# RG-LRU gates as 64-row weight blocks on the two halves of TensorE's rows, in a hybrid decoder layer

## The chip, the cores and the metric

The kernel runs on one core of one Trainium2 chip. The metric is the device time of one execution in microseconds (us). Of the kernel before, three runs took 732.56, 734.33 and 735.61 us, so the median is 734.33 us. The execution that the profiler recorded took 734.08 us, of which the core's span (first to last recorded instruction) is 732.3 us. PE is the matrix engine TensorE, PEld its weight loads, DVE is VectorE, ACT is ScalarE, SP issues DMAs.

## The reference

One decoder layer on 512 tokens with 2048 features: a normalised and modulated input is projected to 4160 columns. Of these, 1024 go through a causal convolution of width 4 and a gated linear recurrence (RG-LRU), others through latent attention; both are multiplied with a SiLU gate, concatenated, projected back and added to the input. Cut to the part that the change touches:

```python
def rg_lru_branch(xr, conv_w, conv_b, w_rg_a, b_rg_a, w_rg_x, b_rg_x, lru_lambda):
    xc = causal_depthwise_conv(xr, conv_w) + conv_b          # 1024 channels
    xb = xc.reshape(B, S, RNN_BLOCKS, RNN_BLOCK)             # 16 blocks of 64 channels
    r = sigmoid(einsum('bshi,hij->bshj', xb, w_rg_a) + b_rg_a)
    i = sigmoid(einsum('bshi,hij->bshj', xb, w_rg_x) + b_rg_x)
    log_a = -LRU_C * r * softplus(-lru_lambda)
    a = exp(log_a)
    b = sqrt(-expm1(2.0 * log_a)) * (i * xc)
    h = linear_recurrence(a, b)                              # h[t] = a[t] h[t-1] + b[t]

def reference(...):
    h = rms_norm(x) * (1 + scale) + shift                    # scale, shift, gate from c
    xr, gr, qc, kvc, kr, ga = split(h @ w_in)
    y_rnn = rg_lru_branch(xr, ...) * silu(gr)
    y_att = mla_branch(qc, kvc, kr, ...) * silu(ga)
    return x + gate * (concat(y_rnn, y_att) @ w_out)
```

The gate weights are block diagonal: 16 blocks of 64 x 64 for r and as many for i, so each channel's gates depend on the 64 channels of its own block.

## The kernel before

Channels lie on the 128 partitions, tokens on the 512 columns of a tile. Every product of float32 matrices is made of three matmuls on values split in two (`mm3`, line 127): high part times high part, high times low, low times high. Splitting a tile costs one copy on ACT (the high part) and one subtraction on DVE (the low part), in `split`, line 120.

The input projection is done in four chunks of the 2048 input features (2, 3, 4 and 7 tiles of 128 features). The last chunk is the stage that the change lies in: the loop over `MORDER[:24]` calls `proj_last` for each of 24 output tiles. One call loads 128 x 896 weights (`wraw`, then split into `whi` and `wlo`, two buffers each in this stage), issues 21 matmuls of 512 columns (14 with `whi`, 7 with `wlo`) into one PSUM bank (`pp`), and DVE adds the bank to the partial sums of the earlier chunks. ACT writes `whi` for the next tile while PE works on the present one, and DVE writes `wlo` behind it.

Between these calls the recurrence is issued in two halves of four channel tiles. `rg_conv` (at n = 4, 5 and n = 9, 10) makes the convolution of a channel tile (`xc`), splits it (`xs`), loads and splits the gate weights (`graw`, `gh`, `gl`: 128 x 256, two block-diagonal 128 x 128 matrices, half of them zeros), makes six matmuls (`pr` and `pi`, one PSUM bank each, on banks 4 to 7 in turn), two sigmoids on ACT (r into the tile's own slot, i into `ig`), and the product `ig` times `xc` on DVE. `rg_decay` (n = 6 and 11) makes the decay with Exp and Tanh, `rg_scan` (n = 7 and 12) a square root and the scan. Sigmoid, Exp/Tanh and Sqrt are each behind an ACT table load, and `tab` keeps these functions in the order in which they are written.

A scheduler orders the instructions of PE, ACT and DVE within the program from its own estimates of time; SP's DMAs stay as written. So gate matmuls stand between projection matmuls at places that the scheduler chose, and ACT's and DVE's queues mix both kinds of work. Each engine works through its own row in order.

Of the kernel before, what the change touches and what calls it, by code (L numbers as in the profile page):

```python
# [12 lines left out]
F32 = mybir.dt.float32  # L13
F32R = mybir.dt.float32r
BF16 = mybir.dt.bfloat16
I32 = mybir.dt.int32
AF = mybir.ActivationFunctionType
# [3 lines left out]
P = 128  # L21
# [29 lines left out]
C_BADA, C_CW, C_CB, C_BA, C_BX, C_LAM, C_QA, C_KVA, NVEC = 0, 48, 80, 88, 96, 104, 112, 116, 120  # L51
# [33 lines left out]
def body(ctx, nc, tc, a):  # L85
# [3 lines left out]
    def act(out, in_, func, **kw):  # L89
        return A.activation(out=out, in_=in_, func=func, **kw)  # L90

    def tab(out, in_, func, **kw):
        if last_tab[0] is None:
            i = act(out, in_, func, **kw)
        else:
            with tc.issue_after(last_tab[0]):
                i = act(out, in_, func, **kw)
        last_tab[0] = i.ins if hasattr(i, "ins") else i
        return i

    def stt(out, in0, scalar, in1, op0, op1, **kw):
        return V.scalar_tensor_tensor(out=out, in0=in0, scalar=scalar, in1=in1, op0=op0, op1=op1, **kw)
# [14 lines left out]
    def tt(o, x, y, op):  # L117
        return V.tensor_tensor(out=o, in0=x, in1=y, op=op)  # L118

    def split(hi, lo, src):  # L120
        act(hi, src, AF.Copy)
        return tt(lo, src, hi.bitcast(F32), ALU.subtract)

    def mm(out, lhsT, rhs, start, stop, **kw):
        PE.matmul(out=out, lhsT=lhsT, rhs=rhs, start=start, stop=stop, **kw)  # L125

    def mm3(out, wh, wl, xh, xl, start, stop, **kw):
        mm(out, wh, xh, start, False, **kw)
        mm(out, wh, xl, False, False, **kw)
        mm(out, wl, xh, False, stop, **kw)  # L130
# [38 lines left out]
    def bank(kind, name):  # L169
        return psp.tile([P, S], F32, tag=f"b{next(cyc[kind])}", name=name)  # L170
# [31 lines left out]
    vec = cst.tile([P, NVEC], F32, name="vec")  # L202
# [347 lines left out]
    rg = rgctx.enter_context(tc.tile_pool(name="rg", bufs=1))  # L550
# [7 lines left out]
    def half(tags, cnt, cache, name):  # L558
        n = cnt[0]
        cnt[0] += 1  # L560
        if n % 2 == 0:
            cache[0] = bigt(tags[(n // 2) % len(tags)], name)
        return cache[0][:, n % 2]
# [3 lines left out]
    def tmp(name):  # L567
        return rg.tile([P, S], F32, tag="t", name=name, bufs=4)

    def rg_conv(m):  # L570
        w = lambda t: vec[:, C_CW + 8 * t + m:C_CW + 8 * t + m + 1]
        x = slot[XR + m]
        xc = half(XC, xcn, xcc, "xc")
        act(xc, x, AF.Identity, scale=w(3), bias=vec[:, C_CB + m:C_CB + m + 1])
        for s in (1, 2, 3):
            stt(xc[:, s:S], x[:, 0:S - s], w(3 - s), xc[:, s:S], ALU.mult, ALU.add)
        xs = rg.tile([P, 2, S], F32R, tag="xs", name="xs", bufs=2)
        xh, xl = xs[:, 0], xs[:, 1]
        split(xh, xl, xc)
        raw = rg.tile([P, 256], F32, tag="graw", name="graw", bufs=2)  # L580
        DMA.dma_start(out=raw, in_=a["wrg"][m])
        gh = rg.tile([P, 256], F32R, tag="gh", name="gh", bufs=2)
        gl = rg.tile([P, 256], F32R, tag="gl", name="gl", bufs=2)
        split(gh, gl, raw)
        pr = bank("aux", "pr")
        mm3(pr, gh[:, 0:P], gl[:, 0:P], xh, xl, True, True)
        pi = bank("aux", "pi")
        mm3(pi, gh[:, P:2 * P], gl[:, P:2 * P], xh, xl, True, True)
        tab(x, pr, AF.Sigmoid, bias=vec[:, C_BA + m:C_BA + m + 1])
        ig = tmp("ig")  # L590
        tab(ig, pi, AF.Sigmoid, bias=vec[:, C_BX + m:C_BX + m + 1])
        tt(xc, ig, xc, ALU.mult)
        return xc

# [104 lines left out]
    for n, m in enumerate(MORDER[:24]):  # L699
# [13 lines left out]
        if n in (4, 5):  # L713
            for t in (2 * n - 8, 2 * n - 7):
                xcs[t] = rg_conv(t)
# [6 lines left out]
        if n in (9, 10):  # L722
            for t in (2 * n - 14, 2 * n - 13):
                xcs[t] = rg_conv(t)
# [395 lines left out]
def _layout(x, c, positions, w_ada, b_ada, w_in, conv_w, conv_b, w_rg_a, b_rg_a, w_rg_x, b_rg_x, lru_lambda,  # L1120
            q_a_norm, w_uq, kv_a_norm, w_ukv, q_norm_nope, q_norm_rope, k_norm_nope, k_norm_rope, w_out):
    f = np.float32
    con = np.ascontiguousarray
    d = {}
    d["x"] = con(x[0].T).reshape(NK, P, S)
    d["xtok"] = con(x[0]).reshape(NT, P, D)
    d["c"] = con(c).reshape(4, S)
    d["pos"] = con(positions[0].reshape(NT, P).T)
    d["ada"] = con(w_ada[0].T).reshape(48, P, D)
    w = w_in[0]  # L1130
    cols = np.concatenate([w[:, 0:2048], w[:, 2048:2560], w[:, 2560:3072], w[:, 3136:4160]], axis=1)
    c4 = cols.reshape(NK, P, 32, P)
    c4 = c4[:, :, list(MORDER)]
    for ci, (k0, kc) in enumerate(CHUNKS):
        G = GROUP[ci]
        t = c4[k0:k0 + kc].reshape(kc, P, 32 // G, G, P)
        d[f"win{ci}"] = con(t.transpose(2, 1, 3, 0, 4)).reshape(32 // G, P, G * kc * P)
    kc = CHUNKS[0][1]
    d["winf"] = con(c4[:kc, :, :NF].reshape(kc, P, NF // 4, 4 * P).transpose(0, 2, 1, 3))
    kr4 = w[:, 3072:3136].reshape(NK, P, 64)  # L1140
    for ci, (k0, kc) in enumerate(CHUNKS):
        d[f"wkr{ci}"] = con(kr4[k0:k0 + kc].transpose(1, 0, 2)).reshape(P, kc * 64)
    g = np.zeros((8, P, 2, P), f)
    for m in range(8):
        for gi, wr in enumerate((w_rg_a[0], w_rg_x[0])):
            for b in range(2):
                g[m, b * 64:(b + 1) * 64, gi, b * 64:(b + 1) * 64] = wr[2 * m + b]
    d["wrg"] = g.reshape(8, P, 256)
    uk = w_ukv[0].reshape(2, 2, P, 4, 2, 2, P)
    t = uk.transpose(3, 0, 2, 1, 5, 4, 6)  # L1150
    d["wuk"] = con(t[:, :, :, :, 0].transpose(0, 2, 1, 3, 4, 5)).reshape(4, P, 1024)
    d["wuv"] = con(t[:, :, :, :, 1].transpose(0, 2, 1, 3, 4, 5)).reshape(4, P, 1024)
    uq = w_uq[0].reshape(2, 2, P, 4, 2, 192).transpose(3, 0, 2, 1, 4, 5)
    d["wqn"] = con(uq[..., 0:128].transpose(0, 2, 1, 3, 4, 5)).reshape(4, P, 1024)
    uq2 = w_uq[0].reshape(4, P, 4, 2, 192).transpose(2, 1, 0, 3, 4)
    d["wqp"] = con(uq2[..., 128:192]).reshape(4, P, 512)
    d["wlast"] = con(w_out[0][15 * P:, NACC * P:(NACC + 4) * P])
    d["wout"] = con(w_out[0].reshape(16, P, 16, P).transpose(2, 1, 0, 3)).reshape(16, P, 2048)
    v = np.zeros((P, NVEC), f)
    v[:, 0:48] = b_ada[0].reshape(48, P).T  # L1160
    v[:, C_CW:C_CW + 32] = conv_w[0].reshape(4, 8, P).transpose(2, 0, 1).reshape(P, 32)
    for col, arr in ((C_CB, conv_b), (C_BA, b_rg_a), (C_BX, b_rg_x), (C_LAM, lru_lambda)):
        v[:, col:col + 8] = arr[0].reshape(8, P).T
    for col, arr in ((C_QA, q_a_norm), (C_KVA, kv_a_norm)):
        v[:, col:col + 4] = arr[0].reshape(4, P).T
    d["vec"] = v
    r = np.zeros((P, NROW), f)
    for col, arr in ((R_QN, q_norm_nope), (R_KN, k_norm_nope), (R_QR, q_norm_rope), (R_KR, k_norm_rope)):
        r[:, col:col + arr.shape[1]] = arr[0][None, :]
    r[:, R_IF:R_IF + 32] = INV_FREQ[None, :]  # L1170
    r[:, R_ID:R_ID + P] = np.eye(P, dtype=f)
    r[:, R_MK:R_MK + P] = np.triu(np.full((P, P), -1e30, f), 1)
    d["row"] = r
    return d
# [14 lines left out]
```

## Time and profile before

| | |
|---|---|
| median of 3 runs | 734.33 us (732.56 to 735.61) |
| the profiled execution | 734.08 us, span 732.3 us |
| PE busy | 720.5 us, 98% of the span |
| PE weight loads busy | 597.4 us, 82% |
| DVE busy | 527.1 us, 72% |
| ACT busy | 353.6 us, 48% |
| gate matmuls | 48 of 128 x 512, from 255.6 to 299.6 us |
| gate sigmoids | 16 of 128 x 512, from 256.5 to 301.8 us |

A timeline row of the profile has the start in us, the length in us, the engine, the source line, the operation, what it writes and reads, its shape and how many such instructions were merged into the row; square brackets hold the idle time of the engine before the row and what ended it. Matmuls are pipelined: each is recorded with its latency (0.39 us at 512 columns), and the time that it costs is the distance of two starts. In a windows row each engine has its busy time in the stretch and its number of instructions.

### The profile page before, as it was taken

To read this page: it belongs to the slowest core of one execution; us is meant where nothing else is said; L and a number is where in the kernel's file an instruction comes from. 1 tells how busy PE (TensorE), PEld (TensorE's weight loads), DVE (VectorE), ACT (ScalarE), POOL (GpSimd) and SP (SyncE) were. 2 spreads that over 40 slices of the span, in tenths; PEclk is the share of its full clock that TensorE was granted. 3 is DMA by queue.
4 is the path that set the end of the run, shared out by engine and by line. 5 is a ranking of instruction groups with operands and counts; after the bars stand their busy time and mean duration, and the time that the engine had idled before them with its cause. 6 is when DMAs were issued, how large, how long until landed. Compare 5 with 4: busy or idle time off the path is not lost.

```text
span 732.3 us, 10065 instructions
## 1 busy us (share of the span) xinstructions
PE 720.5 (98%) x3625; PEld 597.4 (82%) x3626; DVE 527.1 (72%) x949; ACT 353.6 (48%) x728; POOL 29.4 (4%) x34
## 2 busy tenths in 40 slices
PE   9799999999999999999999999999999999999998
PEld 4588887788888888878888888888888877888887
DVE  2997878899998889897765566567686677783232
ACT  7366322231223489875545568677465434222221
POOL 0000000000000000001011111111120100000000
PEclk9899999999999999999999999999999999999999
DMA  8998366987822322223243315213433799774330
GB/s 308 391 409 323 116 242 225 368 325 272 332 80 79 127 80 81 81 79 101 82 134 95 93 59 202 62 55 118 130 127 100 239 333 296 241 228 138 114 94 29
DMA packets 46002, 127.94 MB, mean 175 GB/s; under 512 B 5373, under 2 KB 9341, under 8 KB 42369
## 3 DMA queue, kind: packets, MB, share of 16 engines
q1 hardware_dynamic: 38896, 106.34, 42.1%
q10 hardware_dynamic: 7056, 20.97, 8.5%
q8 instruction: 28, 0.46, 0.2%
q14 instruction: 22, 0.17, 0.1%
HBM read 123.10 MB, written 4.19 MB: 174 GB/s over the span
## 4 chain that ended last, share of the span: by engine, by line
PE 79%; DMA 7%; DVE 5%; ACT 5%; issue 3%; SPq 1%; POOLq 0%; POOL 0%; ACTq 0%; DVEq 0%
PE pp L125 36%; PE oa L125 23%; PE sc L125 4%; PE uwqn L125 3%; PE uwuk L125 3%; DMA ada<-in_ada 3%; PE uwuv L125 3%; DMA xtok<-in_xtok 2%; PE op L125 2%; PE uqp L125 2%; DMA wraw<-in_wout 1%; PE tp L894 1%; ACT pj L90 1%; PE tq L794 1%; DVE xc L118 1%
## 5 line engine op out<-in xcount | busy, mean ns | idle before, releaser
L125 PE MATMUL pp<-h,whi 128*128 128x512 f32 x992 | 242.0, 391 | 0.5 <-ACT h L90 0.5
L90 ACT ACTIVATE whi<-wraw 128x512 fp32r<-128x512 f32 (+4 forms) x172 | 126.8, 740 | 207.5 <-PE pp L125 69.7
L125 PEld LDWEIGHTS pp<-h,whi 128*128 128x128 f32 x992 | 184.8, 188 | 39.7 <-ACT whi L90 1.0
L118 DVE TENSOR_TENSOR wlo<-wraw,whi 128x512 fp32r<-128x512 f32 (+4 forms) x172 | 141.0, 822 | 67.6 <-ACT whi L90 35.9
L125 PE MATMUL pp<-h,wlo 128*128 128x512 f32 x496 | 127.2, 390 | 1.5 <-DVE wlo L118 1.5
L125 PEld LDWEIGHTS pp<-h,wlo 128*128 128x128 f32 x496 | 92.7, 188 | 21.6 <-DVE wlo L118 2.5
L125 PE MATMUL oa<-yh,whi 128*128 128x512 f32 (+1 forms) x272 | 102.4, 384 | 0.1
L125 PE MATMUL oa<-yl,whi 128*128 128x512 f32 (+1 forms) x272 | 102.3, 380 | 0.0
L276 DVE CUSTOM_DVE_ANT_0 ada<-ada,cb,vec 128x2048 f32<-128x2048 f32 (+1 forms) x32 | 70.7, 2211 | 11.3 <-DMA ada<-in_ada 11.3
L118 DVE TENSOR_TENSOR pj<-pp,pj 128x512 f32<-128x512 f32 x96 | 64.0, 683 | 13.8 <-PE pp L125 13.2
L125 PE MATMUL oa<-yh,wlo 128*128 128x512 f32 (+1 forms) x272 | 71.8, 380 | 0.0
L125 PEld LDWEIGHTS oa<-yl,whi 128*128 128x128 f32 x272 | 51.3, 189 | 8.9 <-DVE yl L118 0.2
L125 PEld LDWEIGHTS oa<-yh,whi 128*128 128x128 f32 x272 | 51.3, 189 | 8.8 <-ACT yh L90 0.3
L125 PEld LDWEIGHTS oa<-yh,wlo 128*128 128x128 f32 x272 | 49.1, 188 | 9.1
L90 ACT ACTIVATE h<-x,mod 128x512 fp32r<-128x512 f32 x14 | 10.2, 730 | 33.4 <-DVE mod L276 17.7
L125 PE MATMUL sc<-kT,qT 128*128 128x128 f32 (+3 forms) x96 | 22.8, 332 | 1.1 <-ACT kT L90 1.1
L90 ACT ACTIVATE pj<-pp 128x512 f32<-128x512 f32 x32 | 17.4, 611 | 9.3 <-PE pp L125 9.3
L90 ACT ACTIVATE pr<-sc,nm 128x128 f32<-128x128 f32 (+3 forms) x32 | 16.7, 521 | 10.6 <-DVE nm L886 10.4
L276 DVE CUSTOM_DVE_ANT_0 ada<-ada,cbo,vec 128x1024 f32<-128x1024 f32 x16 | 20.5, 1279 | 1.2 <-DMA ada<-in_ada 1.2
L229 POOL TENSOR_TENSOR hs<-hs,mhalf 128x8 f32<-128x8 f32 x12 | 21.2, 1768 | 1.0
L276 DVE CUSTOM_DVE_ANT_0 ada<-ada,cbo,modh 128x1024 f32<-128x1024 f32 x16 | 20.5, 1279 | 0.9 <-DMA ada<-in_ada 0.9
L125 PE MATMUL uwuv<-whi,kvt 128*128 128x256 f32 x80 | 20.8, 284 | 0.0
(222 smaller groups left out, 1001.6 us busy)
## 6 DMA issues: line engine op xcount, KB each, us to landing
ada<-in_ada SPq DMA_DIRECT2D x28, 1024.0 KB, 7.9
ada<-in_ada ACTq DMA_DIRECT2D x32, 512.0 KB, 4.9
wraw<-in_wout SPq DMA_DIRECT2D x59, 256.0 KB, 3.6
wraw<-in_win SPq DMA_DIRECT2D x22, 512.0 KB, 6.5
wraw<-in_win SPq DMA_DIRECT2D x24, 448.0 KB, 3.2
wraw<-in_win SPq DMA_DIRECT2D x16, 384.0 KB, 4.2
xtok<-in_xtok SPq DMA_DIRECT2D x8, 512.0 KB, 7.3
xo<-in_x SPq DMA_DIRECT2D x16, 256.0 KB, 4.9
```

Source lines behind the costliest of these rows:

```text
L90: return A.activation(out=out, in_=in_, func=func, **kw)
L118: return V.tensor_tensor(out=o, in0=x, in1=y, op=op)
L125: PE.matmul(out=out, lhsT=lhsT, rhs=rhs, start=start, stop=stop, **kw)
L229: G.tensor_tensor(out=out, in0=out, in1=mhalf[:, :n], op=ALU.pow)
L276: ttr_last[0] = V.tensor_tensor_reduce(out=t, in0=t, in1=cv, op0=ALU.mult, op1=ALU.add, scale=1.0, scalar=vec[:, C_BADA + j:C_BADA + j + 1 ...
L794: PE.transpose(tp[:, d * 256 + i2 * P:d * 256 + (i2 + 1) * P], kt[u][:, q * P:(q + 1) * P], ident)
L894: PE.transpose(tp[:, j * P:(j + 1) * P], pr[:, j * P:(j + 1) * P], ident)
```

## The change

The gate weights of a channel tile become 128 x 128: partitions 0 to 63 hold block 2m with its r columns and i columns side by side, partitions 64 to 127 hold block 2m+1 with its i columns first and then r. The six matmuls of a tile now have 64 rows of weights each: three on rows 0 to 63 of the array into bank `pg0` (r of the lower channels on partitions 0 to 63, i of the same channels on 64 to 127), three on rows 64 to 127 into bank `pg1` (i below, r above). They are issued in turn, one for each half. The two sigmoids of 128 partitions become four of 64 partitions; those of i read one half of the partitions and write the other, so that i lies again on its channels. The bias column of i is rolled by 64 partitions for that. Loads, splits and buffers of the gate weights are half as wide.

```diff
--- before.py
+++ after.py
@@ -577,18 +577,20 @@
         xs = rg.tile([P, 2, S], F32R, tag="xs", name="xs", bufs=2)
         xh, xl = xs[:, 0], xs[:, 1]
         split(xh, xl, xc)
-        raw = rg.tile([P, 256], F32, tag="graw", name="graw", bufs=2)
+        raw = rg.tile([P, P], F32, tag="graw", name="graw", bufs=2)
         DMA.dma_start(out=raw, in_=a["wrg"][m])
-        gh = rg.tile([P, 256], F32R, tag="gh", name="gh", bufs=2)
-        gl = rg.tile([P, 256], F32R, tag="gl", name="gl", bufs=2)
+        gh = rg.tile([P, P], F32R, tag="gh", name="gh", bufs=2)
+        gl = rg.tile([P, P], F32R, tag="gl", name="gl", bufs=2)
         split(gh, gl, raw)
-        pr = bank("aux", "pr")
-        mm3(pr, gh[:, 0:P], gl[:, 0:P], xh, xl, True, True)
-        pi = bank("aux", "pi")
-        mm3(pi, gh[:, P:2 * P], gl[:, P:2 * P], xh, xl, True, True)
-        tab(x, pr, AF.Sigmoid, bias=vec[:, C_BA + m:C_BA + m + 1])
+
+        pb = [bank("aux", f"pg{b}") for b in range(2)]
+        L, U = slice(0, 64), slice(64, P)
+        for n, (g, v) in enumerate(((gh, xh), (gh, xl), (gl, xh))):
+            for ps, h in zip(pb, (L, U)):
+                mm(ps, g[h], v[h], n == 0, n == 2)
         ig = tmp("ig")
-        tab(ig, pi, AF.Sigmoid, bias=vec[:, C_BX + m:C_BX + m + 1])
+        for o, c, ps, src, dst in ((x, C_BA, pb[0], L, L), (ig, C_BX, pb[0], U, L), (x, C_BA, pb[1], U, U), (ig, C_BX, pb[1], L, U)):
+            tab(o[dst], ps[src], AF.Sigmoid, bias=vec[src, c + m:c + m + 1])
         tt(xc, ig, xc, ALU.mult)
         return xc
 
@@ -1140,12 +1142,9 @@
     kr4 = w[:, 3072:3136].reshape(NK, P, 64)
     for ci, (k0, kc) in enumerate(CHUNKS):
         d[f"wkr{ci}"] = con(kr4[k0:k0 + kc].transpose(1, 0, 2)).reshape(P, kc * 64)
-    g = np.zeros((8, P, 2, P), f)
-    for m in range(8):
-        for gi, wr in enumerate((w_rg_a[0], w_rg_x[0])):
-            for b in range(2):
-                g[m, b * 64:(b + 1) * 64, gi, b * 64:(b + 1) * 64] = wr[2 * m + b]
-    d["wrg"] = g.reshape(8, P, 256)
+    g = np.stack([w_rg_a[0], w_rg_x[0]], axis=1).reshape(8, 2, 2, 64, 64)
+    g = np.stack([g[:, 0], g[:, 1, ::-1]], axis=1)
+    d["wrg"] = con(g.transpose(0, 1, 3, 2, 4)).reshape(8, P, P)
     uk = w_ukv[0].reshape(2, 2, P, 4, 2, 2, P)
     t = uk.transpose(3, 0, 2, 1, 5, 4, 6)
     d["wuk"] = con(t[:, :, :, :, 0].transpose(0, 2, 1, 3, 4, 5)).reshape(4, P, 1024)
@@ -1161,6 +1160,7 @@
     v[:, C_CW:C_CW + 32] = conv_w[0].reshape(4, 8, P).transpose(2, 0, 1).reshape(P, 32)
     for col, arr in ((C_CB, conv_b), (C_BA, b_rg_a), (C_BX, b_rg_x), (C_LAM, lru_lambda)):
         v[:, col:col + 8] = arr[0].reshape(8, P).T
+    v[:, C_BX:C_BX + 8] = np.roll(v[:, C_BX:C_BX + 8], 64, axis=0)
     for col, arr in ((C_QA, q_a_norm), (C_KVA, kv_a_norm)):
         v[:, col:col + 4] = arr[0].reshape(4, P).T
     d["vec"] = v
```

On PE, tiles 0 and 1 of the recurrence stand together in both kernels. `pr`, `pi` are the banks before, `pg0`, `pg1` those for the lower and upper half of the rows; the row before:

```order
L125 MATMUL pr_2093<-xs_2084,gh_2089 128x512 x2
L125 MATMUL pr_2093<-xs_2084,gl_2090 128x512
L125 MATMUL pi_2097<-xs_2084,gh_2089 128x512 x2
L125 MATMUL pi_2097<-xs_2084,gl_2090 128x512
L125 MATMUL pr_2118<-xs_2109,gh_2114 128x512 x2
L125 MATMUL pr_2118<-xs_2109,gl_2115 128x512
L125 MATMUL pi_2122<-xs_2109,gh_2114 128x512 x2
L125 MATMUL pi_2122<-xs_2109,gl_2115 128x512
```

and of the change:

```order
L125 MATMUL pg0_2093<-xs_2084,gh_2089 128x512
L125 MATMUL pg1_2094<-xs_2084,gh_2089 128x512
L125 MATMUL pg0_2093<-xs_2084,gh_2089 128x512
L125 MATMUL pg1_2094<-xs_2084,gh_2089 128x512
L125 MATMUL pg0_2093<-xs_2084,gl_2090 128x512
L125 MATMUL pg1_2094<-xs_2084,gl_2090 128x512
L125 MATMUL pg0_2120<-xs_2111,gh_2116 128x512
L125 MATMUL pg1_2121<-xs_2111,gh_2116 128x512
L125 MATMUL pg0_2120<-xs_2111,gh_2116 128x512
L125 MATMUL pg1_2121<-xs_2111,gh_2116 128x512
L125 MATMUL pg0_2120<-xs_2111,gl_2117 128x512
L125 MATMUL pg1_2121<-xs_2111,gl_2117 128x512
```

The number of matmuls is the same, twelve; lower and upper half now take turns throughout.

On PE at tile 6 the scheduler places them otherwise. Before:

```order
L125 MATMUL pp_2507<-h11_1468,wlo_2511 128x512
L125 MATMUL pr_2464<-xs_2455,gh_2460 128x512
L125 MATMUL pr_2464<-xs_2455,gl_2461 128x512
L125 MATMUL pi_2468<-xs_2455,gh_2460 128x512
L125 MATMUL pi_2468<-xs_2455,gl_2461 128x512
L125 MATMUL pp_2507<-h12_1563,wlo_2511 128x512
```

and of the change, where `pp` is the projection with all 128 rows:

```order
L125 MATMUL pg0_2476<-xs_2467,gh_2472 128x512
L125 MATMUL pp_2523<-h11_1468,wlo_2527 128x512
L125 MATMUL pg0_2476<-xs_2467,gh_2472 128x512
L125 MATMUL pg0_2476<-xs_2467,gl_2473 128x512
L125 MATMUL pp_2523<-h12_1563,wlo_2527 128x512
L125 MATMUL pg1_2477<-xs_2467,gh_2472 128x512 x2
L125 MATMUL pg1_2477<-xs_2467,gl_2473 128x512
L125 MATMUL pp_2523<-h13_1643,wlo_2527 128x512
```

Here the three matmuls of the lower half and the three of the upper half stand apart, and projection matmuls come between them, so no two neighbours are of different halves. Over all eight tiles the gate matmuls stand in twelve unbroken groups between projection matmuls; nine groups (12, 2, 4, 2, 4, 3, 9, 2 and 4 matmuls) take turns, three (1, 2 and 3) are of one half.

On ACT, from the table load ahead of the sigmoids of tiles 4 and 5 onwards (`xs_2480` before and `xs_2494` after are the high part of tile 7's convolution, `whi` the projection's weights). Before:

```order
L90 ACT_TABLE_LOAD
L90 ACTIVATE pj4_320<-pr_2378,vec_81 128x512
L90 ACTIVATE ig_2387<-pi_2382,vec_81 128x512
L90 ACTIVATE xs_2455<-xc_2450 128x512
L90 ACTIVATE pj5_321<-pr_2403,vec_81 128x512
L90 ACTIVATE gh_2485<-graw_2483 128x256
L90 ACTIVATE ig_2412<-pi_2407,vec_81 128x512
L90 ACTIVATE xs_2480<-xc_2450 128x512
L90 ACTIVATE lsq_2415<-pj21_337 128x512
L90 ACTIVATE lat21_2418<-pj21_337,vec_81 128x512
L90 ACTIVATE whi_2577<-wraw_2575 128x896
L90 ACTIVATE whi_2622<-wraw_2620 128x896
```

and of the change:

```order
L90 ACT_TABLE_LOAD
L90 ACTIVATE pj4_320<-pg0_2386,vec_81 64x512
L90 ACTIVATE ig_2394<-pg0_2386,vec_81 64x512
L90 ACTIVATE pj4_320<-pg1_2387,vec_81 64x512
L90 ACTIVATE ig_2394<-pg1_2387,vec_81 64x512
L90 ACTIVATE gh_2499<-graw_2497 128x128
L90 ACTIVATE pj5_321<-pg0_2413,vec_81 64x512
L90 ACTIVATE ig_2421<-pg0_2413,vec_81 64x512
L90 ACTIVATE pj5_321<-pg1_2414,vec_81 64x512
L90 ACTIVATE ig_2421<-pg1_2414,vec_81 64x512
L90 ACTIVATE lsq_2427<-pj21_337 128x512
L90 ACTIVATE xs_2494<-xc_2462 128x512
```

Four sigmoids became eight, and all eight now stand ahead of tile 7's `xs`; tile 6's `xs` and one `lat` moved ahead of the table load.

## Rows read from the trace of the kernel before

**Rows 1.** The page: busy time, share of the span and instructions by engine.
```profile
PE 720.5 (98%) x3625; PEld 597.4 (82%) x3626; DVE 527.1 (72%) x949; ACT 353.6 (48%) x728; POOL 29.4 (4%) x34
```

**Rows 2.** Busy time by stretch, in the last projection chunk.
```profile
core 0: us, PE busy (x) PEld busy (x) DVE busy (x) ACT busy (x) POOL busy (x), PEclk, DMA share, GB/s
...
265.00:275.00 10.00, 10.00 (x46) 8.29 (x45) 7.79 (x12) 8.56 (x14) 0.00 (x0) 1.00 0.24 72
275.00:285.00 10.00, 10.00 (x46) 8.29 (x45) 9.37 (x14) 9.97 (x16) 0.00 (x0) 1.00 0.33 98
285.00:295.00 10.00, 10.00 (x46) 8.29 (x45) 9.78 (x15) 9.97 (x18) 0.00 (x0) 1.00 0.26 88
...
315.00:325.00 10.00, 8.93 (x43) 6.99 (x42) 8.83 (x12) 7.10 (x11) 0.00 (x0) 1.00 0.16 48
```

**Rows 3.** Timeline of PE: first and after the last gate matmul, tiles 0 and 1.
```profile
255.61 0.61 PE L125 MATMUL pr<-xs,gh 128*128 128x512 f32 x2
...
258.33 0.84 PE L125 MATMUL pp<-h,whi 128*128 128x512 f32 x3
```

**Rows 4.** Timeline of PE: 256-column matmuls, each with its own weights.
```profile
401.02 0.28 PE L125 MATMUL uwuv<-whi,kvt 128*128 128x256 f32 x1
401.14 0.28 PE L125 MATMUL uwuv<-whi,lat 128*128 128x256 f32 x1
```

**Rows 5.** Timeline of PE: eight matmuls with 4 weight rows between 128-row ones.
```profile
7.92 0.38 PE L125 MATMUL junk_ps<-junk 128*128 128x512 bf16 x1
8.23 1.21 PE L125 MATMUL cb_ps<-c4h,sel 4*128 4x512 f32 x4
9.28 1.08 PE L125 MATMUL cb_ps<-c4l,sel 4*128 4x512 f32 x4
10.29 0.44 PE L375 MATMUL xps<-row,xtok 128*128 128x128 f32 x2
10.57 0.38 PE L125 MATMUL junk_ps<-junk 128*128 128x512 bf16 x1
```

**Rows 6.** Timeline of PE: the last of those eight matmuls.
```profile
9.97 0.39 PE L125 MATMUL cb_ps<-c4l,sel 4*128 4x512 f32 x1
```

**Rows 7.** Timeline of ACT: a copy of 512 columns on 4 partitions.
```profile
4.34 0.61 ACT L90 ACTIVATE c4h<-c 4x512 fp32r<-4x512 f32 x1
```

**Rows 8.** Timeline of ACT around the sigmoids.
```profile
268.50 0.69 ACT L90 ACTIVATE pj<-pr,vec 128x512 f32<-128x512 f32 x1 [0.17 <-PE pr L125]
...
288.77 1.28 ACT L90 ACT_TABLE_LOAD   x1
290.07 0.69 ACT L90 ACTIVATE pj<-pr,vec 128x512 f32<-128x512 f32 x1
290.65 0.68 ACT L90 ACTIVATE ig<-pi,vec 128x512 f32<-128x512 f32 x1
...
293.19 0.64 ACT L90 ACTIVATE xs<-xc 128x512 fp32r<-128x512 f32 x1
293.71 0.64 ACT L90 ACTIVATE lsq<-pj 128x512 f32<-128x512 f32 x1
...
294.85 0.96 ACT L90 ACTIVATE whi<-wraw 128x896 fp32r<-128x896 f32 x1
296.61 0.96 ACT L90 ACTIVATE whi<-wraw 128x896 fp32r<-128x896 f32 x1 [0.81 <-PE pp L125]
299.50 0.73 ACT L90 ACTIVATE lat<-pj,vec 128x512 fp32r<-128x512 f32 x1 [1.94 <-DVE pj L118]
```

**Rows 9.** Timeline of PE: the projection tile behind the gates, and PE's one wait.
```profile
299.81 0.39 PE L125 MATMUL pp<-h,whi 128*128 128x512 f32 x1
...
324.38 1.89 PE L125 MATMUL pp<-h,wlo 128*128 128x512 f32 x7 [1.07 <-DVE wlo L118]
```

**Rows 10.** Splits of the gate weights (ns min/median/max, first and last start).
```profile
L90 ACT ACTIVATE gh<-graw x8: 402/408/420, 239.0 to 292.3; 128x256 fp32r<-128x256 f32 x8
L118 DVE TENSOR_TENSOR gl<-graw,gh x8: 416/422/426, 239.5 to 294.8; 128x256 fp32r<-128x256 f32 x8
```

## The prediction

> **What bounds the kernel now.** I read the page's busy times first: PE is busy for 98% of the span, ACT for 48% [rows 1]. So a microsecond taken off PE counts, as long as PE then still finds its inputs. Next the stretches of the last projection chunk, where the recurrence lies: PE fills each up to 315 us at the full granted clock (1.00, 2.4 GHz), but ACT is busy for 9.97 of 10 us in two stretches running, and DVE for 9.4 and 9.8 [rows 2]. Here the two helpers have no time left, which the 48% hides. Last the timelines: of PE for the distance of two starts, of ACT for what stands ahead of an input that PE wants. PE's one wait of the stage is for a `wlo` of DVE, 1.07 us at 324 us [rows 9].
>
> **PE's matmuls.** Twelve gate matmuls lie between 255.61 and 258.33 us: 2.72 us, 0.227 us each [rows 3]. All 48 cost 48 x 0.227 = 10.9 us, and as PE never waits there, this is time of the end. After the change there are again 48 matmuls of 512 columns. Whether two of different halves run side by side, no row of before shows, since none uses the upper rows alone. The bounds: not at all, 0.227 us for each; fully, 0.227 us for a pair. Between lies a limit that rows do show: each matmul brings its own weights, and where matmuls have only 256 columns, they start 0.12 us apart, each with a weight load [rows 4]. If loads stay one behind the other, a pair costs 2 x 0.12 = 0.24 us. I take that, so matmuls that take turns start 0.12 us apart, and the last of a group streams its 0.227 us. Of the twelve groups in PE's row, nine take turns, with 42 matmuls: (42 - 9) x 0.12 + 9 x 0.227 = 6.0 us. The three groups of one half have 6: 1.4 us. Together 7.4 us, so **-3.5 us**.
>
> The Trainium skill, TensorE: Matmul & The Clock Gate, "Measured speedup vs the span model", has packed matmuls take one matmul's time plus about 4 ns per further tile. By it a pair would be 0.23 us and the groups some 1 us cheaper in all; no run here shows it yet.
>
> **The switches of shape.** Each group of 64-row matmuls has 128-row ones on both sides: 12 x 2 = 24 switches. The trace has one such place, with 4-row weights. From the last 128-row matmul (7.92 us) to the fifth 4-row one (9.28 us) lie 1.36 us; five in a row would take 5 x 0.23 = 1.15 us (three 4-row distances, 9.28 to 9.97 us, are 0.69 us). So 0.21 us go at the entry. The copy that it needs ended at 4.95 us [rows 7], and no other wait explains it. At the way out, from 9.97 to 10.57 us are 0.60 us, where 0.23 and two transposes at 0.12 us would be 0.47: 0.13 us [rows 4 to 6]. I take the mean, 0.17 us: 24 x 0.17 = **+4.1 us** (3.1 to 5.0). From below the bound is zero, if halves of 64 rows mix with full ones without a stop.
>
> The Trainium skill, TensorEngine Tiling (Array Packing), "Key Properties", speaks against the change: changing the tiling mode, not just the tile, drains the engine. The 0.13 and 0.21 us above agree with it. Without that rule the sum would end 4.1 us lower.
>
> The new waits of PE for PE (first matmul of a bank) are for matmuls at least 37 instructions back: nothing.
>
> **ACT.** Sixteen sigmoids of 128 partitions become 32 of 64. Fewer partitions aren't cheaper: a copy of 512 columns takes 0.61 us on 4 partitions [rows 7] and 0.64 us on 128 [rows 8]. Two sigmoids start 0.58 us apart [rows 8], so ACT gets 16 x 0.58 = 9.3 us more; `gh` at half width gives back up to 0.1 us of each 0.41, eight times [rows 10]. For tiles 0 to 3 ACT still has gaps; the last is 0.17 us at 268.50 us [rows 8], and behind it ACT is full. So the last tile's two more sigmoids, 1.2 us, are carried into the full stretch. Then the place on which PE hangs: from the table load to tile 7's `xs` ACT took 293.19 - 288.77 = 4.4 us. In the new order there stand the load (1.30), eight sigmoids (4.64), `gh` (0.30, an estimate from its 0.41) and `lsq` (0.52): 6.8 us, 2.4 more. `xs` would end at 293.83 + 1.2 + 2.4 = 297.4 us, and the `whi` behind it about 0.9 us later, 298.3 us. PE wants `xs` for tile 7's first pair, ahead of the projection tile that started at 299.81 us [rows 9]; tile 7's six matmuls (1.4 us) now lie behind that point, so it comes at about 299 us. Slack of around 1 us: hidden, but barely. What stands behind `xs` has ACT's own gaps of 0.81 and 1.94 us [rows 8] to catch up. If the cover is gone, each us late costs a us. I take **+0.5 us** (0 to 2.4). The old wait at 324 us may grow by 0.8 (3.6 carried, less the two gaps) or go (-1.1), as ACT's order is new there; I take it as staying.
>
> **DVE and DMA.** `gl` at half width is below its 0.42 us eight times [rows 10]: DVE gains a little, off PE's path. The product `ig` times `xc` waits for the fourth sigmoid, about 1.2 us later, and feeds the scan, which no matmul of this stretch reads. The weight DMA is half as large at the same place of SP's row. Nothing for both.
>
> **Sum.** On the profiled execution's own time: 734.08 - 3.5 + 4.1 + 0.5 = **735.2 us**. It lies 0.25 us below the median of 734.33, well within the 3 us over which the three runs spread, so I keep it.
>
> **Rivals.**
> 1. The halves don't run side by side, and the change doesn't do what it is built for: each matmul stays at 0.227 us, the switches and ACT's work stay. 734.08 + 4.1 + 0.5 = 738.7 us, slower. For it: no row shows two matmuls at once. Against: the upper half has its own weights, rows and bank.
> 2. The switches are free, as 64 rows are a simple half: 734.08 - 3.5 + 0.5 = 731.1 us. For it: the only row on switches is of another shape, at the program's start. Against: both its ends show a cost.
> 3. As 2, and ACT's new order also takes away the wait at 324 us: 734.08 - 3.5 - 1.1 = 729.5 us, faster.
> 4. ACT becomes the bound: the carried 1.2 us, 2.4 us ahead of `xs`, and four more sigmoids for tiles 6 and 7 (2.3 us) are 5.9 us; once `xs` is later than its slack of 1 us, PE pays the rest. 734.08 + 0.6 + 4.9 = 739.6 us, slower. For it: ACT at 9.97 of 10 us. Against: two gaps of 2.75 us together right behind.
>
> **How the numbers follow.** Forecast 50%, rival 1 19%, rival 2 16%, rival 3 8%, rival 4 7%. About 0.5% (3.7 us) is what a measurement of this kernel can tell from no change. Rival 3 and the low end of rival 2 are faster: 0.10. Rival 4, most of rival 1 and the forecast's upper end are slower: 0.23. The rest, 0.67, is the same. The likeliest case alone runs from 732.6 (switches at 3.1, no wait of ACT's, the old wait gone) to 737.4 us (switches at 5.0, ACT at 1.8). The range takes in rivals 1 and 2 and leaves out rival 3 and most of rival 4: 730.9 to 739.3 us.
>
> **What would show it.** In the changed profile's PE timeline, `pg0` and `pg1` starting 0.12 us apart (0.227 is rival 1), and about 0.17 us lost at each side of a group (no loss is rival 2). Twelve matmuls of tiles 0 and 1 with both their switches should take 1.9 us instead of 2.7. A wait of PE for ACT at tile 7's `xs` or the `whi` behind it beyond 1 us is rival 4. The forecast is wrong if PE waits elsewhere for more than 2 us that it did not wait before.

## The result, and the profile after

The changed kernel took 737.58 us, the median of nine runs (733.86 to 739.45); the kernel before, run beside it, 734.08 us (nine runs, 732.56 to 737.42). The ratio is 1.0043, with a 95% interval of 1.0025 to 1.0061: about 3 us slower, where 735.2 us was forecast. The profiled execution took 738.07 us, 3.99 us more than that of before, with a span of 736.3 us.

The page of the changed kernel, busy time, share of the span and instructions by engine, as in [rows 1]:

```profile
PE 722.8 (98%) x3625; PEld 593.9 (81%) x3626; DVE 525.9 (71%) x949; ACT 364.8 (50%) x744; POOL 29.5 (4%) x34
```

PE is busy for 2.3 us more, although its pairs run side by side (next view). ACT has 16 instructions and 11.2 us more; it is idle for half of the span, but full in this one stage [rows 2].

The timeline of PE in the changed kernel, tiles 0 and 1, where [rows 3] has twelve matmuls in a row:

```profile
256.39 0.73 PE L125 MATMUL pg<-xs,gh 64*128 64x512 f32 x4
256.96 0.40 PE L125 MATMUL pg<-xs,gl 64*128 64x512 f32 x2
257.20 0.62 PE L125 MATMUL pg<-xs,gh 64*128 64x512 f32 x4
257.66 0.40 PE L125 MATMUL pg<-xs,gl 64*128 64x512 f32 x2
257.98 3.47 PE L125 MATMUL pp<-h,whi 128*128 128x512 f32 x14
```

From 256.96 to 257.20 us pass 0.24 us for two matmuls, and from 257.20 to 257.66 us 0.46 us for four: a pair costs what one matmul cost before. The starts of single matmuls in the same trace are 0.004 us apart within a pair. The first pair starts 0.318 us after the projection matmul ahead of it, the second 0.335 us after the first, and the two first projection matmuls behind the group come 0.323 and 0.338 us apart, where 0.227 to 0.23 us is the undisturbed distance. So a group of 64-row matmuls costs about 0.41 us for going in and out of its shape.

Further on, PE's timeline has the waits:

```profile
295.91 0.50 PE L125 MATMUL pg<-xs,gh 64*128 64x512 f32 x1
296.33 0.49 PE L125 MATMUL pp<-h,wlo 128*128 128x512 f32 x1
296.76 0.49 PE L125 MATMUL pg<-xs,gh 64*128 64x512 f32 x1
...
301.41 0.80 PE L125 MATMUL pg<-xs,gh 64*128 64x512 f32 x2 [1.72 <-ACT xs L90]
302.25 5.93 PE L125 MATMUL pp<-h,whi 128*128 128x512 f32 x14
...
331.77 2.60 PE L125 MATMUL pk<-h,wkhl 128*128 128x512 f32 x10 [1.12 <-DVE wkhl L118]
```

PE stands still for 1.72 us until ACT has written `xs` of tile 7. Then fourteen matmuls take 5.93 us, where the fourteen at 257.98 us, also behind a gate group, take 3.47 us (view above). The pair ahead of them takes 0.84 us to the next start, a single pair at 264.78 us only 0.43. The windows (busy time of each engine, then the granted clock, the DMA share and GB/s) tell why, and should be set beside [rows 2]:

```profile
core 0: us, PE busy (x) PEld busy (x) DVE busy (x) ACT busy (x) POOL busy (x), PEclk, DMA share, GB/s
285.00:295.00 10.00, 10.00 (x48) 7.75 (x47) 8.97 (x14) 9.94 (x16) 0.00 (x0) 1.00 0.27 81
295.00:305.00 10.00, 8.24 (x25) 4.74 (x24) 9.93 (x15) 9.84 (x17) 0.00 (x0) 0.79 0.09 28
...
300.75:307.50 6.75, 6.04 (x14) 4.41 (x15) 5.46 (x8) 5.53 (x9) 0.00 (x0) 0.50 0.39 119
```

From 300.75 to 307.50 us the granted clock is 0.50, the lower of TensorE's two levels, 1.2 GHz; the kernel before stays at 1.00 here. And ACT's timeline shows what `xs` stood behind, as in [rows 8]:

```profile
293.11 1.28 ACT L90 ACT_TABLE_LOAD   x1
294.40 0.68 ACT L90 ACTIVATE pj<-pg,vec 64x512 f32<-64x512 f32 x1
295.10 0.69 ACT L90 ACTIVATE ig<-pg,vec 64x512 f32<-64x512 f32 x1
295.81 0.68 ACT L90 ACTIVATE pj<-pg,vec 64x512 f32<-64x512 f32 x1
...
300.21 0.63 ACT L90 ACTIVATE lsq<-pj 128x512 f32<-128x512 f32 x1
300.75 0.61 ACT L90 ACTIVATE xs<-xc 128x512 fp32r<-128x512 f32 x1
```

Half sigmoids start 0.70 us apart, where full ones started 0.58 us apart. About half of the delay of `xs` had come about earlier, in the sigmoids of tiles 0 to 3. This is the first table load behind them, before and then after:

```profile
270.09 1.28 ACT L90 ACT_TABLE_LOAD   x1
```

```profile
274.26 1.28 ACT L90 ACT_TABLE_LOAD   x1
```

It comes 4.17 us later. Of these, 0.69 us are an offset of the whole execution (next paragraph) and 3.5 us are the longer work of ACT.

Set side by side by the n-th projection matmul, the two traces give most of the account. Ahead of the first gate, where nothing is changed, after is 0.69 us later than before; such an offset between two executions is no effect. At the 1,100th projection matmul (293.7 us of before) it is 0.60 us earlier. So 1.3 us were gained, 0.5 of them only because two gate matmuls fewer lie ahead of that point. At the 1,140th (305.0 us) it is 5.94 us later. Of the 6.5 us in between, 1.8 are the wait with its late step, 2.9 are matmuls at the lower clock (5.93 instead of 3.47 us, and 0.84 instead of 0.43), and 1.8 are gate groups: twelve matmuls in five groups, where before has ten in three. So the stage lost 5.2 us, and of that the gate matmuls with their switches are only about 0.5 us: 11.4 us for all eight tiles against 10.9. At the end 3.96 us are left, with the offset. Of the waits outside the gates, the one of 1.07 us at 324 us [rows 9] has its equal at 331.77 us, and one of 1.1 us for a `kT` of ACT in the attention part (588.8 us of before) is gone; there and just behind it the distance falls from 5.63 to 3.96 us, and no run ties this to the change.

### The profile page after: what moved, and what is told of

It is laid out like the page before. It is cut to its first block, busy times and chain, and to the rows that moved or that the text cites. A ratio compares the mean times of both kernels' runs of the same rounds, so it can differ in the third digit from the quotient of the medians.

```text
span 736.3 us, 10093 instructions
## 1 busy us (share of the span) xinstructions
PE 722.8 (98%) x3625; PEld 593.9 (81%) x3626; DVE 525.9 (71%) x949; ACT 364.8 (50%) x744; POOL 29.5 (4%) x34
## 4 chain that ended last, share of the span: by engine, by line
PE 55%; ACT 2%; DVE 1%; issue 0%
PE oa L125 24%; PE pp L125 11%; PE sc L125 4%; PE uwuv L125 3%; PE uwqn L125 3%; PE uwuk L125 3%; PE op L125 2%; PE uqp L125 2%; PE tp L896 1%; PE tq L796 1%; ACT pj L90 1%; PE pk L125 0%; PE tqe L851 0%; ACT L90 0%; ACT a L90 0%
## 5 line engine op out<-in xcount | busy, mean ns | idle before, releaser
L125 PE MATMUL pp<-h,whi 128*128 128x512 f32 x992 | 245.3, 394 | 0.6 <-ACT h L90 0.6
L90 ACT ACTIVATE PT<-tp 128x128 f32<-128x128 f32 (+3 forms) x32 | 13.9, 435 | 13.9 <-PE tp L896 11.4
```

## The experiments

Two theories stood at first. A: the PE part is about even or a small gain, and ACT's longer work in its full stretch makes the loss, by the wait and by what follows from it. B: the loss comes from PE itself, from the shape of the matmuls, the switches or the clock. All ratios are against the kernel before, run on the same chip beside each.

**ACT's part alone: e1_act_halves.** The matmuls stay as before, each sigmoid is done in two halves in place.

```diff
-        tab(x, pr, AF.Sigmoid, bias=vec[:, C_BA + m:C_BA + m + 1])
-        tab(ig, pi, AF.Sigmoid, bias=vec[:, C_BX + m:C_BX + m + 1])
+        for o, c, ps, h in ((x, C_BA, pr, L), (ig, C_BX, pi, L), (x, C_BA, pr, U), (ig, C_BX, pi, U)):
+            tab(o[h], ps[h], AF.Sigmoid, bias=vec[h, c + m:c + m + 1])
```

> The kernel before with its full 128-row gate matmuls; only the sixteen sigmoids are made in halves of 64 partitions, each written to the partitions it is read from. Theory A (the loss comes from ACT: its doubled sigmoids push back an input that PE then waits for): a part of the loss shows without any 64-row matmul, ratio to before 1.002 to 1.006, and a wait of PE for ACT of over 1 us. Rival B (the loss comes from PE's switches between 128-row and 64-row matmuls): ratio 1.000, no new wait. The changed kernel's half sigmoids start 0.70 us apart, before 0.58: if halves as such cost this, 0.70 here too; if crossing the partitions does, 0.58.

Measured: 739.99 us, ratio 1.0082 (1.0061 to 1.0102), above the range of Theory A. The halves alone cost more than the whole change. ACT's timeline and then PE's in this kernel:

```profile
298.00 0.69 ACT L90 ACTIVATE pj<-pr,vec 64x512 f32<-64x512 f32 x1
298.58 0.67 ACT L90 ACTIVATE ig<-pi,vec 64x512 f32<-64x512 f32 x1
299.27 0.68 ACT L90 ACTIVATE pj<-pr,vec 64x512 f32<-64x512 f32 x1
299.86 0.67 ACT L90 ACTIVATE ig<-pi,vec 64x512 f32<-64x512 f32 x1
```

```profile
302.56 0.73 PE L125 MATMUL pr<-xs,gh 128*128 128x512 f32 x2 [0.88 <-ACT pj L90]
...
304.63 3.68 PE L125 MATMUL pp<-h,whi 128*128 128x512 f32 x15 [0.41 <-ACT whi L90]
```

Two sigmoids on the same half start 0.58 to 0.59 us apart, as full ones do; one that goes to the other half starts 0.69 us after the one ahead. In the change each sigmoid differs from the one ahead either in the half that it reads or in the half that it writes, and its row above has 0.70 to 0.71 us at every step. PE waits for ACT here too, with 128-row matmuls, six times between 300 and 341 us for 3.9 us in all, and the clock stays at full: these waits need no 64-row matmul.

**PE's part alone: e2_pe_halves.** The 64-row matmuls as in the change, two full sigmoids per tile. Moving back is left out, so i and r of the upper channels are exchanged in what follows.

```diff
-        for o, c, ps, src, dst in ((x, C_BA, pb[0], L, L), (ig, C_BX, pb[0], U, L), ...
-            tab(o[dst], ps[src], AF.Sigmoid, bias=vec[src, c + m:c + m + 1])
+        tab(x, pb[0], AF.Sigmoid, bias=vec[:, C_BA + m:C_BA + m + 1])
+        tab(ig, pb[1], AF.Sigmoid, bias=vec[:, C_BX + m:C_BX + m + 1])
```

> The change on PE alone: 64-row gate matmuls on two halves, but two full-width sigmoids per tile as before, on the banks as they are (r and i of the upper channels are left exchanged, the moving back is left out). Theory A: no wait of PE for ACT, ratio 0.997 to 1.001 (about 26 slots of 0.23 us and ten groups with 0.40 us of switches are 10.0 us against 10.9). Rival B: the loss stays, ratio 1.003 or more.

Measured: 731.54 us, ratio 0.9974 (0.9958 to 0.9989): a gain of about 1.9 us. Its windows:

```profile
core 0: us, PE busy (x) PEld busy (x) DVE busy (x) ACT busy (x) POOL busy (x), PEclk, DMA share, GB/s
...
295.00:305.00 10.00, 10.00 (x45) 7.75 (x45) 8.60 (x13) 8.38 (x13) 0.00 (x0) 1.00 0.29 93
```

No wait, full clock. In its trace the ten groups cost about 10.0 us, switches included, against 10.9 us in before. That is 0.9 us of the gain; the rest can't be placed in one trace. With e1 this speaks for Theory A: PE's part can gain, and ACT's part loses. But the scheduler has also ordered this program otherwise. A pair, or a matmul alone, is one start: here are ten groups with 25 starts, in the change twelve with 28, which cost it about 11.4 us. So of the distance between e2 and the change some 1.4 us are the placement of the gates, and with the change's own placement PE's part gains nothing.

**The order within a group: e3_no_turns.** The three matmuls of one half, then the three of the other.

```diff
-        for n, (g, v) in enumerate(((gh, xh), (gh, xl), (gl, xh))):
-            for ps, h in zip(pb, (L, U)):
+        for ps, h in zip(pb, (L, U)):
+            for n, (g, v) in enumerate(((gh, xh), (gh, xl), (gl, xh))):
```

> The changed kernel with the three matmuls of the lower half first and then the three of the upper half. If halves run side by side only where neighbours are of different halves, a tile takes 4 to 5 slots of 0.23 us instead of 3: about 10 slots more, +2.3 us on the changed kernel, ratio to before about 1.007. If the order doesn't matter, as the changed kernel, 1.004.

Measured: 739.32 us, ratio 1.0066 (1.0047 to 1.0086), 1.7 us above the change by the medians, though the two intervals overlap. PE's timeline, the twelve matmuls of tiles 0 and 1 and then the late wait:

```profile
256.04 0.74 PE L125 MATMUL pg<-xs,gh 64*128 64x512 f32 x4
256.61 0.40 PE L125 MATMUL pg<-xs,gl 64*128 64x512 f32 x2
...
257.64 1.20 PE L125 MATMUL pp<-h,whi 128*128 128x512 f32 x4
...
301.75 0.51 PE L125 MATMUL pg<-xs,gh 64*128 64x512 f32 x2 [1.78 <-ACT gh L90]
302.59 3.73 PE L125 MATMUL pp<-h,whi 128*128 128x512 f32 x9 [0.34 <-ACT whi L90]
```

In PE's row of this program three matmuls of one half stand ahead of three of the other, and still they ran in pairs, 0.01 us apart: the twelve take 1.60 us, as with turns (1.59 us, from 256.39 to 257.98 us in the change). So the turns are not what makes the pairs, and that each engine works through its own row in order holds for PE only within one half. The wait for ACT is as long as in the change, and the clock fell here as well (0.50 from 302.2 to 305.6 us). The trace has one group more (13) and the further wait of 0.34 us; whether the rest of the 1.7 us is real is not shown.

**Taking `xs` out from behind the sigmoids: e4_xs_first.** The sigmoids of tiles 4 to 7 are issued behind the splits of tiles 6 and 7. The diff is cut to the place of the call; `rg_gate` holds the four sigmoids and the product.

```diff
-                xcs[t] = rg_conv(t)
+                held[t] = rg_conv(t)
+            if n == 10:
+                for t in range(4, 8):
+                    with tc.issue_after(held[7][3]):
+                        xcs[t] = rg_gate(t, *held[t][:3])
```

> The changed kernel with the sigmoids of tiles 4 to 7 written behind the convolutions and splits of tiles 6 and 7, so that ACT makes tile 7's xs first. The scheduler then puts the gates into 8 groups instead of 12. Theory A: the 1.7 us wait for xs is gone, and the lowered clock behind it; with fewer groups PE's gates take 8.9 us instead of 10.9 before: ratio 0.996 to 1.000. Rival B: only the four groups less count (4 x 0.4 = 1.6 us off the changed kernel), ratio 1.002.

Measured: 738.96 us, ratio 1.0077 (1.0052 to 1.0102). The expectation missed. PE's timeline:

```profile
297.09 0.72 PE L125 MATMUL pg<-xs,gh 64*128 64x512 f32 x2 [0.42 <-ACT ig L90]
...
298.50 0.73 PE L125 MATMUL pg<-xs,gh 64*128 64x512 f32 x2 [0.44 <-ACT ig L90]
...
299.89 1.22 PE L125 MATMUL pg<-xs,gh 64*128 64x512 f32 x2 [0.40 <-ACT ig L90]
```

The wait for `xs` is gone, but the gates now wait for their PSUM banks, which ACT's sigmoids of the earlier tiles still hold. These waits part the three matmuls of one half from the three of the other, so the last twelve, which stand in the same order as in e3, take twelve starts and not six: pairs need both halves ready. And the granted clock is 0.50 from 299.3 to 306.1 us here as well. The wait had only been moved. That fits ACT's amount of work as the cause, rather than one instruction in a bad place, but alone it doesn't show it, as the groups changed with it.

**Less work on ACT: e5_pool_relief, and its control e6_before_pool.** The first tap of the convolution and the square in the decay go from ACT to POOL, in the changed kernel (e5) and in the kernel before (e6).

```diff
-        act(xc, x, AF.Identity, scale=w(3), bias=vec[:, C_CB + m:C_CB + m + 1])
+        G.tensor_scalar(out=xc, in0=x, scalar1=w(3), scalar2=vec[:, C_CB + m:C_CB + m + 1], op0=ALU.mult, op1=ALU.add)
-        act(a2, al, AF.Square)
+        G.tensor_tensor(out=a2, in0=al, in1=al, op=ALU.mult)
```

> The changed kernel with eight first convolution taps (xc, 0.70 us of ACT each) and eight squares (a2, 0.52 us each) made on the idle POOL instead of ACT: 9.8 us less for ACT, which is most of what the halves added. Theory A (ACT's queue is what turns a gain on PE into a loss): PE waits for ACT by under 0.5 us around the gates, the clock stays at its upper level there, ratio to before 0.994 to 0.999. Rival C (not ACT's amount of work but the bare order or the switches): ratio stays 1.003 or more. POOL's durations for 128 x 512 are not in any trace; if they are above 3 us, DVE waits for POOL and the ratio is above 1.000 as well, with that wait in the profile.

> Control for the run with POOL: the kernel before with the same sixteen operations on POOL. ACT was full there only from 270 to 296 us and PE had one wait of 1.1 us in the stage, so at most that wait can go: ratio 0.997 to 1.000. If this alone gains as much as the changed kernel with POOL, the gate matmuls have no part in the gain.

Measured: e5 737.25 us, ratio 1.0020 (0.9999 to 1.0041); e6 738.91 us, ratio 1.0059 (1.0033 to 1.0084). Both expectations missed: e5 is not below 1, with waits of PE for ACT well above 0.5 us, and e6 is slower than the kernel before. POOL's groups in e5 (busy time, mean ns, idle time before and what ended it) and PE's waits there (total, times, longest):

```profile
L574 POOL TENSOR_SCALAR xc<-pj,vec 128x512 f32<-128x512 f32 x8 | 15.7, 1958 | 260.3 <-DVE pj L118 251.5 <-issue 4.6 <-ACT xs L90 4.2
```

```profile
PE pp L125 <- ACT whi L90: 1.9, 2, 1.4
PE pg L125 <- ACT xs L90: 1.4, 1, 1.4
PE pg L125 <- DVE xs L118: 0.7, 1, 0.7
```

POOL takes 1.96 us for the tap, and DVE waits for it (3.2 us in all in e5, 2.9 us in e6), so the relief costs something in both kernels. What can be read is the order of the two: given the same help, the 64-row gates have the lower ratio, where without help they have the higher one. The intervals of the two overlap slightly, so this alone would not settle it.

**The change of half: e7_by_half.** The half sigmoids of two tiles are sorted, so that every second one stays on its half. The diff is cut to the loop.

```diff
+        for k in range(4):
+            for m in ts_:
+                x, xc, pb, ig = held[m]
+                o, c, ps, src, dst = (...)[k]
+                tab(o[dst], ps[src], AF.Sigmoid, bias=vec[src, c + m:c + m + 1])
```

> The changed kernel with the eight sigmoids of two tiles sorted by halves: both tiles' first, then both tiles' second, and so on. Half sigmoids started 0.70 us apart where the partitions read or written changed and 0.58 where they stayed. So four of eight should start 0.58 apart: 0.5 us less per pair of tiles, 2 us less of ACT in all, and the gates fall into fewer groups. Theory A: the wait at the second half shrinks but ACT still has some 11 us more than before: ratio 1.001 to 1.004. If it is not the changing of partitions, all stay at 0.70.

Measured: 737.33 us, ratio 1.0036 (1.0015 to 1.0057), as the change. ACT's timeline:

```profile
296.76 1.26 ACT L90 ACTIVATE pj<-pg,vec 64x512 f32<-64x512 f32 x2
298.03 1.26 ACT L90 ACTIVATE ig<-pg,vec 64x512 f32<-64x512 f32 x2
```

Two sigmoids take 1.27 us from start to start instead of 1.40, so the extra 0.11 us is indeed that of the change of half. But a tile's banks are now held until its partner's are done, PE waits 2.0 us for `ig`, and nothing is won.

**Moving the halves without ACT: e8_dma_back and e9_dma_actq.** Two full sigmoids per tile with mixed biases, and three SBUF-to-SBUF transfers of 64 x 512 put the halves where they belong: on POOL's queue in e8, on ACT's in e9. The diff leaves out the mixing of the biases and one more buffer.

```diff
+        y, ig = tmp("y"), tmp("ig")
+        tab(x, pb[0], AF.Sigmoid, bias=vec[:, C_BA + m:C_BA + m + 1])
+        tab(y, pb[1], AF.Sigmoid, bias=vec[:, C_BX + m:C_BX + m + 1])
+        G.dma_start(out=ig[L], in_=x[U])       # e9: A.dma_start, three times
+        G.dma_start(out=ig[U], in_=y[L])
+        G.dma_start(out=x[U], in_=y[U])
```

> 64-row gates as in the change, but two full-width sigmoids of a tile (as in e2_pe_halves), and the halves put back by three SBUF-to-SBUF transfers of 128 KB on POOL's queue, so that neither ACT nor DVE gets an instruction more; one buffer more for the third tile. Theory A (the change loses its gain only through the ACT time of the four half sigmoids; PE's part is worth about -2 us, as e2_pe_halves had it): PE waits for no ACT row in 290 to 305 us, granted clock stays at full, 0.9965 to 1.0000 of before (the transfers' few us of latency lie behind the gates, where only decay and scan wait for them). Rival B (moving the halves costs time wherever it is put, since tiles stay longer in their buffers and DVE's queue stops at the multiply that waits for the transfer, with the splits of weights behind it): 1.002 to 1.008, PE waiting for whi, wlo or xs from DVE.

> The same with the three transfers issued from ACT's queue, in place of POOL's. Theory A: like e8_dma_back unless the issues hold ACT: 0.9970 to 1.0020. Rival B: 1.003 to 1.010, since ACT's queue also stops at each issue until the sigmoid has ended and the buffer is free, so that evacuations behind it come later.

Measured: e8 733.46 us, ratio 0.9990 (0.9974 to 1.0006); e9 734.25 us, ratio 0.9995 (0.9979 to 1.0012), both as Theory A had it. Both compute the whole layer. The windows of e8, and its transfers (KB each, median us from issue to landing):

```profile
core 0: us, PE busy (x) PEld busy (x) DVE busy (x) ACT busy (x) POOL busy (x), PEclk, DMA share, GB/s
...
285.00:295.00 10.00, 10.00 (x48) 7.11 (x45) 10.00 (x15) 8.38 (x14) 2.59 (x5) 1.00 0.53 159
295.00:305.00 10.00, 10.00 (x48) 7.74 (x47) 6.83 (x11) 7.99 (x12) 3.61 (x7) 1.00 0.49 138
```

```profile
ig<-pj POOLq DMA_DIRECT2D x8, 128.0 KB, 3.2
ig<-y POOLq DMA_DIRECT2D x8, 128.0 KB, 3.1
pj<-y POOLq DMA_DIRECT2D x8, 128.0 KB, 2.3
```

PE is full and at the full clock in both stretches, the second of which holds the change's wait, and the transfers' 2 to 3 us lie where only the product with `xc` and the decay wait for them (DVE stood 2.2 us for them in all). The interval of e8 lies below that of the change (1.0025 to 1.0061) and holds 1, so this version undoes the loss and is not shown to beat the kernel before. Whether the distance to e2's 0.9974 is real stays open, since these two intervals overlap.

## Why the prediction held for PE and missed for ACT, point by point

- **The bound.** PE at 98% with two full helpers in this stage held: of the 13 us that ACT was given more, 1.7 us came out as a wait of PE, with the lowered clock behind it.
- **PE's matmuls, -3.5 us.** Too little. The step that failed is "if loads stay one behind the other": matmuls of two halves start 0.004 us apart, each with its own weight load, and pairs 0.23 us. The changed row has 12 groups with 28 starts (22 in the nine groups that take turns, a last one alone counted as one, and 6 in the three of one half): 28 x 0.227 = 6.4 us, so -4.5. The rule of the Trainium skill's TensorE: Matmul & The Clock Gate, "Measured speedup vs the span model", that stood beside this step is what the trace shows, 4 ns for the further tile.
- **The switches, +4.1 us.** Twelve groups at 0.41 us are +4.9 us, 0.20 us a switch instead of 0.17. Sign and place were right, and it lies within the range of 3.1 to 5.0. On each side two starts are late by about 0.1 us. The twelve matmuls of tiles 0 and 1 with both their switches take 1.8 us, where 1.9 was forecast.
- **PE in sum, +0.6.** The trace gives about +0.5, as the two misses of about 1 us nearly cancel, which is luck; e2 with ten groups gives -0.9 by its trace and -1.9 by its times. Rivals 1 (not side by side) and 2 and 3 (switches free) are excluded by the same rows.
- **ACT, +0.5 us (0 to 2.4).** This is the term that was mis-sized. "Two sigmoids start 0.58 us apart [rows 8], so ACT gets 16 x 0.58 = 9.3 us more" took the distance from sigmoids on the same partitions; those of the change start 0.70 us apart, 32 x 0.70 - 16 x 0.58 = 13.1 us more in all. So 3.5 us and not 1.2 were carried into the full stretch (the table load at 274.26 us, without the offset), and the table load ahead of the sigmoids of tiles 4 and 5 came at 293.11 us, 4.3 us later than before. From this load to the start of `xs` passed 7.64 us instead of 6.8, so `xs` ended at 301.36 us and not 297.4; PE stood there from 299.69 us. "Hidden, but barely" became a wait of 1.72 us, and a wait beyond 1 us at this place is the prediction's own sign of rival 4.
- **What the prediction had no term for.** From within that wait on the clock was granted at 0.50 for 6.75 us, which cost 2.9 us, more than the wait itself. "Each us late costs a us" was too low a price.
- **The old wait.** It was taken as staying, and it stayed in size: 1.07 us at 324 us before [rows 9], 1.12 us at 331.77 us after, on another tile.
- **The rivals.** The mechanism that came true is rival 4's, ACT as the bound, given 7%. Its 739.6 us priced a wait of 4.9 us; the stage lost 5.2 us, from a shorter wait and a lower clock, and part came back further on. The time lies between it and the forecast. That it lies within 730.9 to 739.3 us is in part luck: the range reaches so far up for rival 1 (738.7 us), which did not come about, and the likeliest case by itself ended at 737.4 us.

In the Trainium skill, TensorEngine Tiling (Array Packing), "PSUM Bottleneck" says that packing speeds up TensorE but not the emptying of PSUM, which may become the bottleneck. The runs agree in part: in e2, with as many sigmoids as before, packing kept its gain (-1.9 us by the ratio), and what became the bottleneck was ACT's emptying only once it was doubled (e1, +6.0 us without any packing). The doubling comes from this kernel's layout.

**What stays open.** Why the clock fell. It did in four kernels with 64-row groups and waits of PE for ACT between 296 and 302 us (the change, e3, e4, e7). It did not in e1 (128-row gates, a wait of 0.88 us here and one of 1.6 us further on), in e2 and e8 (64-row gates, no such wait there), nor in e5 (64-row gates, a wait of 1.4 us at 293.8 us). No run takes the wait's length and the shape of the matmuls apart, so what the 2.9 us hang on isn't shown.

## What to carry to other kernels

Before work is packed on one engine, count the instructions that the result's new layout needs on the engine that reads it: here PE could win one to two microseconds at best (e2), and putting the halves back cost ACT thirteen, in a stage in which it had few to give. Count the groups too that the matmuls fall into: each cost 0.41 us for its two changes of shape. An engine at 50% of the span can be full in the very stage of a change; take its busy share from that stretch, and the price of an instruction from rows with the same partitions. Where only the place of data is wrong, a transfer on an idle queue can do it without an instruction of PE, ACT or DVE, as long as its 2 to 3 us are waited for by nothing urgent.

## What the runs showed of the hardware that was not expected

- ACT: of two sigmoids of 512 columns in a row, the second starts 0.58 us after the first on the same partitions (64 or 128 of them) and 0.69 to 0.70 us after it where the other half's partitions follow. The instructions themselves are 0.68 us long, so a change of half takes away the overlap of 0.11 us. The Trainium skill's ScalarE: Activation LUTs, "What ACT_TABLE_LOAD costs", gives an overlap of about 93 ns for ACT instructions in a row; the rows agree for the same partitions and not for a change of half.
- PE: two halves of the rows ran side by side also where the program has three matmuls of the one ahead of three of the other (e3: twelve in 1.60 us), but not where PE had to wait between the threes (e4: twelve starts for the last twelve).
- PE: the stop between shapes spreads over four starts of a group (+0.09, +0.10 us going in, +0.10, +0.11 us coming out), so a group of a single pair costs 0.63 us, nearly three projection matmuls.
- The 6.75 us at a granted clock of 0.50 cost 2.9 us, more than one and a half times the wait of 1.72 us within which they began.
